# A decoder layer: the feed-forward norm vector is multiplied onto token rows instead of weights, a second pair of token tiles is turned by VectorE through DRAM, and differences are made in place

## The chip, the cores and the metric

The kernel runs on one core of a Trainium2 chip. The metric is the device time of one execution in microseconds. The engines have short names in the profile: PE is TensorE, DVE VectorE, ACT ScalarE, POOL GpSimd, SP SyncE; PEld are the weight loads of PE. SP issues nearly all transfers between DRAM and on-chip memory (SBUF); PE writes to PSUM, its own result memory.

## What is computed

One layer of a decoder over 1024 tokens of 1024 channels, in float32: a mixer (sparse attention of eight heads beside a short convolution) and a feed-forward part. The change lies in the feed-forward part and in what prepares it:

```python
mixed = jnp.concatenate([rms_norm(attn_out, g_out[l, :ATTN_WIDTH]),
                         rms_norm(conv_out, g_out[l, ATTN_WIDTH:])], axis=-1)
x = x + mixed @ w_o[l]
h = rms_norm(x, g_ffn_norm[l])
x = x + jnp.square(jax.nn.relu(h @ w_up[l])) @ w_down[l]
```

`rms_norm(x, g)` divides each token's row by its root mean square and multiplies channel by channel with `g`. Since `h @ w_up` sums over channels, `g_ffn_norm` may stand on the rows of `x` or on the rows of `w_up`. The matrix `w_up` is 1024 x 4096.

## The kernel before

**Tiles and stages.** Tokens are cut in eight tiles of 128, numbered 0 to 7. The stages are: the input projection (tiles `zp`, up to 139 us), the convolution part (`zX`, `zZ`, `zW`, up to 254 us), the convolution's share of the output projection (`wc`, up to 312 us, beside the first scores), attention tile by tile in the order 3, 2, 1, 0, 4, 5, 7, 6 (`ORDER`), the up projection with its square (545 to 880 us) and the down projection (to the end). Each float32 product is made of three fast ones: both operands are split in a rounded part and a rest (`hi` and `lo`, `copy_act` on ACT and a subtraction on DVE or POOL), and `mm3` issues three matmuls.

**Attention.** For each token tile and each of two groups, `scores` lets PE write pieces `s_` to two PSUM banks; DVE reduces each piece to `pt` with its minimum `nm` (an instruction pair that order rows call ISA), which frees the bank for the next piece. POOL and ACT weigh `pt`; PE transposes it (`tp`), ACT and DVE split it (`ph`, `pl`), and PE multiplies it with the values (`ot`). The keys come from DRAM as `kn00`, `kn10`, `kn01`, `kn11` (second digit: first or second half of the tokens), are rounded to `KH` by ACT, and their rests `KL` are made by DVE. The values `vs` and `vw` are 1024 KB each.

**The rows for the feed-forward part.** `finish` (L1476) ends a token tile: it adds the output projection `wa` to the residual row tile `y` (`yacc[tb]`, 128 x 1024), squares it for the norm, and scales it by `rffn`, one number per token. The up projection is a fast product of 2 x 2 blocks with seven products in place of eight. Its seven operands on the token side, `B11`, `B21`, `T1`, `T2`, `T3`, `B22`, `T4`, are halves of the rows of tokens 0 to 3 ("early") and 4 to 7 ("late") and their differences; `mate` pairs token tile 4 with 0, 5 with 1 and so on. Each must lie with channels on partitions, so each half row must be turned. `turn` (L1567) does this with four PE transposes of 128x128 to PSUM, from where ACT and DVE split it. For a pair in `BY_DRAM` (before: tiles 0 and 4), `finish` has DVE turn blocks of 32x32 of the whole row, writes it to DRAM (`t_d`) and reads it back in four pieces, so that it comes back turned; `side` (L1580) then only splits it, out of SBUF. The last token tile, 6, is handled in `second_half` (L1687): its row `ylast` is scaled to two half tiles `xn`.

**Norm vector.** `up_raw` (L1609) loads two of the 32 column blocks of `w_up` (`wu`, 1024 KB) and has ACT scale each of its eight row blocks by `g_ffn_norm`, which lies channel by partition in `cols`.

**What sets the order.** Nothing is issued in the order of the code. Class `Plan` records every operation, and `schedule` places them on the engines by a list schedule with priorities; these come from a backward pass (`latest`), and `best` shakes them once for each number in `SEEDS`: `shaken` moves the due times of the operations in one stretch of 5 to 40 us by random amounts. The result is one fixed order for each engine, with semaphores between engines. A new `SEEDS` therefore gives a new order for nearly everything.

Of the kernel before, what the change touches and what calls it, by code (L numbers as in the profile page):

```python
# [39 lines left out]
BY_DRAM = (0,)  # L40
# [1854 lines left out]
```

## Time and profile before

| | |
|---|---|
| median of 3 runs | 1191.03 us (1188.57 to 1192.53) |
| profiled execution | 1190.73 us |
| its span, first to last instruction | 1189.0 us |
| granted clock of PE, mean | 0.997 |
| data moved by the DMA engines | 161.28 MB |

The page gives busy times by engine. The span of a profiled execution is a little shorter than its time, by what lies ahead of the first instruction and behind the last one. Rows of groups read: engine, operation, tile written, tiles read, shape, count, and durations. In a view of one tile the three numbers are the least, the median and the greatest duration in nanoseconds. In a view of waits they are the total, the number of waits and the longest, in microseconds.

### The profile page before, as it was taken

How to read it: one execution, taken by the hardware profiler on the slowest of the kernel's cores; microseconds unless marked ns; L12 is line 12 of the kernel's file. 1: busy time of each engine (PE TensorE's matmuls, PEld its weight loads, DVE VectorE, ACT ScalarE, POOL GpSimd, SP SyncE). 2: the span in 40 equal slices, each digit the busy share in tenths (PEclk: the TensorE clock that was granted, in tenths of full speed). 3: DMA queues.
4: the chain of work that ended last, by engine and by line, in shares of the span. 5: the costliest groups of instructions: out<-in, count | busy, mean ns of one | idle time of the engine just before them, and what ended most of it. 6: DMA issues, size and time to landing. Idle time of an engine off the chain costs nothing.

```text
span 1189.0 us, 18003 instructions
## 1 busy us (share of the span) xinstructions
PE 1176.9 (99%) x5766; PEld 979.4 (82%) x5766; DVE 916.3 (77%) x1827; ACT 700.7 (59%) x1550; POOL 722.9 (61%) x663
## 2 busy tenths in 40 slices
PE   9999999999999999999999999999999999999998
PEld 7888878887878888888788888888888888888887
DVE  8868877785789999998985664554478979887875
ACT  7877635453689988888855554546345444444441
POOL 1544400022266554545878888787799999888971
PEclk9999999999999999999999999999999999999999
DMA  9845521268121101104045445353469545453513
GB/s 342 207 140 169 176 56 48 71 137 249 45 72 46 45 28 63 55 18 141 20 170 193 134 158 186 116 185 113 171 223 388 147 145 175 162 169 100 175 45 141
DMA packets 115102, 161.28 MB, mean 136 GB/s; under 512 B 21472, under 2 KB 68960, under 8 KB 115008
## 3 DMA queue, kind: packets, MB, share of 16 engines
q1 hardware_dynamic: 108752, 152.44, 39.8%
q10 hardware_dynamic: 5520, 5.28, 1.3%
q0 software_dynamic: 736, 2.43, 0.7%
q8 instruction: 45, 0.74, 0.2%
q14 instruction: 49, 0.40, 0.1%
HBM read 111.87 MB, written 48.23 MB: 135 GB/s over the span
## 4 chain that ended last, share of the span: by engine, by line
PE 89%; DVE 4%; ACT 4%; DMA 2%; issue 1%; SPq 0%; POOL 0%; POOLq 0%; ACTq 0%
PE X L273 28%; PE Z L273 18%; PE zp L273 9%; PE zX L273 5%; PE ot L273 5%; PE tp L273 4%; PE wa L273 3%; PE W L273 3%; PE zZ L273 3%; PE wc L273 2%; PE zW L273 1%; DMA w_raw<-in_w_in_dram 1%; PE hp L273 1%; ACT wu L273 1%; DVE pl L273 1%; DMA vs<-v_ds 1%
## 5 line engine op out<-in xcount | busy, mean ns | idle before, releaser
L273 PE MATMUL X<-we,uu 128*128 128x512 f32 (+1 forms) x726 | 200.9, 388 | 0.0
L273 PE MATMUL Z<-we,uu 128*128 128x512 f32 (+1 forms) x576 | 166.2, 388 | 0.0
L273 PEld LDWEIGHTS X<-we,uu 128*128 128x128 f32 x726 | 136.0, 188 | 28.2 <-DVE y L273 0.2
L273 ACT ACTIVATE uu<-ur 128x512 fp32r<-128x512 f32 x108 | 67.2, 629 | 122.0 <-PE Z L273 72.0
L273 PEld LDWEIGHTS Z<-we,uu 128*128 128x128 f32 x576 | 107.9, 188 | 22.3
L273 DVE TENSOR_TENSOR y<-X,y 128x512 f32<-128x512 f32 x129 | 87.1, 683 | 33.2 <-PE X L273 32.3
L273 ACT ACTIVATE pt<-pt,nm 128x640 f32<-128x640 f32 (+7 forms) x128 | 93.7, 734 | 29.9 <-DVE nm L273 29.7
L273 POOL TENSOR_TENSOR d<-d 128x512 f32<-128x512 f32 x64 | 98.8, 1562 | 8.4 <-DVE d L273 7.8
L273 DVE TENSOR_TENSOR pl<-tp,ph 128x512 fp32r<-128x512 f32 (+1 forms) x148 | 94.8, 656 | 7.5 <-ACT ph L273 7.0
L273 PE MATMUL tp<-ident,pt 128*128 128x128 f32 x528 | 93.0, 274 | 0.0
L273 ACT ACTIVATE ph<-tp 128x512 fp32r<-128x512 f32 (+1 forms) x148 | 80.9, 573 | 15.5 <-PE tp L273 11.5
L273 POOL TENSOR_TENSOR uu<-ur,uu 128x512 fp32r<-128x512 f32 x54 | 80.8, 1501 | 4.9 <-ACT uu L273 4.9
L273 ACT ACTIVATE we<-s 128x512 fp32r<-128x512 f32 x55 | 34.8, 632 | 81.5 <-PE X L273 40.4
L273 DVE TENSOR_TENSOR y<-Z,y 128x512 f32<-128x512 f32 x96 | 64.9, 681 | 21.2 <-PE Z L273 20.7
L273 PEld LDWEIGHTS tp<-ident,pt 128*128 128x128 f32 x528 | 67.5, 141 | 11.2 <-PE tp L273 0.3
L273 POOL MEMSET Qz<- 64x512 f32 x16 | 8.3, 521 | 107.0 <-PE zZ L273 102.9
L273 PE MATMUL zp<-w_lo,hTh 128*128 128x512 f32 (+1 forms) x192 | 67.0, 362 | 0.0
L273 PE MATMUL zp<-w_hi,hTh 128*128 128x512 f32 (+1 forms) x192 | 66.6, 363 | 0.1
L273 PE MATMUL zp<-w_hi,hTl 128*128 128x512 f32 (+1 forms) x192 | 66.0, 360 | 0.0
L273 DVE TENSOR_TENSOR we<-wu,we 128x512 fp32r<-128x512 f32 x38 | 48.5, 1290 | 20.5 <-PE X L273 10.8
L273 POOL TENSOR_TENSOR we<-wd,we 128x512 fp32r<-128x512 f32 x32 | 48.1, 1502 | 24.7 <-ACT we L273 24.3
L273 POOL TENSOR_TENSOR pt<-pt,rr 128x640 f32<-128x640 f32 (+4 forms) x64 | 62.9, 1009 | 0.0
(1353 smaller groups left out, 3611.5 us busy)
## 6 DMA issues: line engine op xcount, KB each, us to landing
u_d<-d SPq DMA_DIRECT2D x112, 256.0 KB, 3.3
ur<-u_d SPq DMA_DIRECT2D x108, 256.0 KB, 2.7
wu<-in_w_up_dram SPq DMA_DIRECT2D x16, 1024.0 KB, 5.8
wd<-in_w_down_dram SPq DMA_DIRECT2D x16, 1024.0 KB, 7.2
xt<-in_x_dram SPq DMA_DIRECT2D x10, 512.0 KB, 5.9
x<-in_x_t_dram SPq DMA_DIRECT2D x16, 256.0 KB, 6.2
w1r<-in_w_cmp_dram SPq DMA_DIRECT2D x16, 256.0 KB, 3.0
q_d<-qn SPq DMA_DIRECT2D x8, 512.0 KB, 3.0
```

Source lines behind the costliest of these rows:

```text
L273: node.do.append(lambda: getattr(engine, method)(*[real(x) for x in a], **{k: real(x) for k, x in kw.items()}))
```

## The change

`g_ffn_norm` comes as a new input `g_rows`, the vector repeated on 128 partitions. The 128 scalings of `wu` are left out. In their place every row is multiplied by the vector: on POOL behind ACT's scaling for token tiles 3 and 2 (in place) and for 1, 0, 4 and 5 (on the way to `yn`), on DVE in one instruction with the scaling for tile 7, and on DVE for tile 6, whose halves of the vector are loaded once more as `gh`. `BY_DRAM` now holds the pairs 1 and 0, so tiles 1 and 5 too go through DVE's transposes and DRAM. For tiles 4, 5 and 7 the difference behind `T2` is written over the one behind `T1`, where a tile `t` of its own was used; its pool `ez` is gone, and several small tiles have two buffers instead of three. `SEEDS` is another list.

```diff
-BY_DRAM = (0,)
+BY_DRAM = (1,0)
...
-SEEDS = (1, 23, 31, 38, 41, 62, 71, 73, 75, 77, 80, 88,
...
+SEEDS = (14, 20, 30, 31, 41, 47, 68, 70, 71, 73, 77, 92,
...
-def trunk_layer(ctx, tc, x, x_t, vectors, w_in, g_qk, w_cmp1, b_cmp1, w_cmp2, b_cmp2,
+def trunk_layer(ctx, tc, x, x_t, vectors, g_rows, w_in, g_qk, w_cmp1, b_cmp1, w_cmp2, b_cmp2,
...
-    cols = cst.tile([P, 68], F32, name="cols")
+    cols = cst.tile([P, 60], F32, name="cols")
...
-    G_MIX, G_FFN, G_OUT, CONV0, PE0 = 0, 8, 16, 24, 36
+    G_MIX, G_OUT, CONV0, PE0 = 0, 8, 16, 28
     def rsqrt(o, ss, n, scale):
-        t = st.tile([P, n], F32, name="rs_t", tag=f"rs{n}")
+        t = st.tile([P, n], F32, name="rs_t", tag=f"rs{n}", bufs=2)
...
-            ss = st.tile([P, G], F32, name="kss")
+            ss = st.tile([P, G], F32, name="kss", bufs=2)
-            ri = st.tile([P, G], F32, name="kri")
+            ri = st.tile([P, G], F32, name="kri", bufs=2)
...
-            ss = st.tile([P, H], F32, name="qss")
+            ss = st.tile([P, H], F32, name="qss", bufs=2)
-            ri = st.tile([P, H], F32, name="qri")
+            ri = st.tile([P, H], F32, name="qri", bufs=2)
...
-            e = st.tile([P, 3 * H], F32, name="ge")
+            e = st.tile([P, 3 * H], F32, name="ge", bufs=1)
...
+        g_ffn = pq.tile([P, D], F32, name="g_ffn", bufs=1)
         def load_wo():
+            nc.sync.dma_start(g_ffn, g_rows)
...
             if tb % 4 not in BY_DRAM:
-                if tb != ORDER[-1]:
+                if tb == ORDER[-2]:
+                    nc.vector.scalar_tensor_tensor(x1, x1, rffn[:, tb:tb + 1], g_ffn, op0=ALU.mult, op1=ALU.mult)
+                elif tb != ORDER[-1]:
                     copy_act(x1, x1, scale=rffn[:, tb:tb + 1])
+                    tt(nc.gpsimd, x1, x1, g_ffn, ALU.mult)
                 return
-            copy_act(yn.rearrange("p (c k t) -> p k c t", c=4, k=KD), x1.rearrange("p (k c t) -> p k c t", c=4, k=KD),
-                     scale=rffn[:, tb:tb + 1])
+            copy_act(x1, x1, scale=rffn[:, tb:tb + 1])
+            tt(nc.gpsimd, yn.rearrange("p (c k t) -> p k c t", c=4, k=KD), x1.rearrange("p (k c t) -> p k c t", c=4, k=KD),
+               g_ffn.rearrange("p (k c t) -> p k c t", c=4, k=KD), ALU.mult)
             nc.vector.transpose(x1, yn)
...
-        ez = pool(e_, "ez")
...
-        def first_turns(tb, t2):
-            tt(nc.vector, t2, rows[tb][1], rows[mate(tb)][0], ALU.subtract)
-            side("T2", tb, t2)
-            side("T1", tb, rows[mate(tb)][0])
+        def first_turns(tb, t2=None):
+            if t2 is None:
+                t2 = rows[mate(tb)][0]
+                side("T1", tb, t2)
+                tt(nc.vector, t2, rows[tb][1], t2, ALU.subtract)
+                side("T2", tb, t2)
+            else:
+                tt(nc.vector, t2, rows[tb][1], rows[mate(tb)][0], ALU.subtract)
+                side("T2", tb, t2)
+                side("T1", tb, rows[mate(tb)][0])
             tt(nc.gpsimd, rows[mate(tb)][1], rows[mate(tb)][1], t2, ALU.subtract)
...
             nc.sync.dma_start(raw, wuv[:, :, q * 2 * P:(q + 1) * 2 * P])
-            for k in range(KD):
-                copy_act(raw[:, k], raw[:, k], scale=cols[:, G_FFN + k:G_FFN + k + 1])
             return {f"A{i + 1}{j + 1}": raw[:, 4 * j:4 * j + 4, i * P:(i + 1) * P] for i in range(2) for j in range(2)}
...
         for tb in late[:-1]:
         for tb in late[:-1]:
-            t = ez.tile([P, 512], F32, name="t", tag="t")
-            first_turns(tb, t if tb % 4 not in BY_DRAM else t.rearrange("p (b k t) -> p b k t", b=4, k=4))
+            first_turns(tb)
             side("T3", tb, rows[tb][0])
...
+        gh = [temp("gh") for _ in range(2)]
+        for i in range(2):
+            nc.sync.dma_start(gh[i], g_rows[:, i * 512:(i + 1) * 512])
-        for o, a in zip(xn, halves(tb)):
-            nc.vector.tensor_scalar(o, a, rffn[:, tb:tb + 1], None, op0=ALU.mult)
+        for o, a, g in zip(xn, halves(tb), gh):
+            nc.vector.scalar_tensor_tensor(o, a, rffn[:, tb:tb + 1], g, op0=ALU.mult, op1=ALU.mult)
...
-_INS = ['x', 'x_t', 'vectors', 'w_in', 'g_qk', 'w_cmp1', 'b_cmp1', 'w_cmp2', 'b_cmp2', 'w_o', 'w_up', 'w_down']
+_INS = ['x', 'x_t', 'vectors', 'g_rows', 'w_in', 'g_qk', 'w_cmp1', 'b_cmp1', 'w_cmp2', 'b_cmp2', 'w_o', 'w_up', 'w_down']
-    a["vectors"] = np.concatenate([a[n].reshape(-1, P) for n in ("g_mix_norm", "g_ffn_norm", "g_out", "conv_w", "pe_cmp")]).T
+    a["vectors"] = np.concatenate([a[n].reshape(-1, P) for n in ("g_mix_norm", "g_out", "conv_w", "pe_cmp")]).T
+    a["g_rows"] = np.tile(a["g_ffn_norm"].reshape(-1), (P, 1))
     return a
```

Since the order is new, it shows best on the engines. The first place is in SP's queue, where the last keys are loaded at the beginning of attention (`kn01`, `kn11` keys, `vs` values, `y` and `xt` residual rows of 512 KB, `qx` queries of 64 KB). Before:

```order
L273 DMA xt_3052<-in_x_dram 128x1024
L273 DMA kn01_2920<-k_d0_211 32x16x64 x3
L273 DMA kn11_2921<-k_d1_210 32x16x64
L273 DMA vs_2942<-v_ds_209 128x8x256
L273 DMA y1_3079<-in_x_dram 128x1024
L273 DMA qx_3082<-q_d_215 32x4x128 x2
L273 DMA kn11_2921<-k_d1_210 32x16x64
L273 DMA kn01_2920<-k_d0_211 32x16x64
L273 DMA qx_3082<-q_d_215 32x4x128
L273 DMA kn11_2921<-k_d1_210 32x16x64 x2
```

And now, at the same place of SP's queue:

```order
L273 DMA kn01_2917<-k_d0_202 32x16x64 x4
L273 DMA xt_3067<-in_x_dram 128x1024
L273 DMA y1_3069<-in_x_dram 128x1024
L273 DMA kn11_2918<-k_d1_201 32x16x64
L273 DMA y0_3091<-in_x_dram 128x1024
L273 DMA qx_3022<-q_d_206 32x4x128
L273 DMA kn11_2918<-k_d1_201 32x16x64 x2
L273 DMA qx_3022<-q_d_206 32x4x128 x3
L273 DMA kn11_2918<-k_d1_201 32x16x64
L273 DMA y4_3148<-in_x_dram 128x1024
L273 DMA vs_2939<-v_ds_200 128x8x256
```

The values `vs` moved from ahead of the last keys to behind them, and the row tile `y0` from behind them to ahead.

The second place is on DVE, at the rests of those keys (`KL`), between the reductions (ISA rows) of the score pieces of token tile 3. Before:

```order
L273 ISA pt_3038,nm_80<-s__3156,d_sw_2937 128x256
L273 ISA nm_80 128x1
L273 TENSOR_TENSOR KL_2938<-kn01_2920,KH1_2939 64x512
L273 TENSOR_TENSOR KL_2938<-kn01_2920,KH0_2940 64x512
L273 TENSOR_TENSOR KL_2938<-kn11_2921,KH1_2939 64x512
L273 TENSOR_TENSOR KL_2938<-kn11_2921,KH0_2940 64x512
L273 ISA pt_3038,nm_80<-s__3176,d_sw_2937,nm_80 128x256
L273 ISA nm_80 128x1
L273 SCALAR_TENSOR_TENSOR y2_2923<-wc_3169,rconv_64,y2_2923 128x512
L273 ISA pt_3038,nm_80<-s__3182,d_sw_2937 128x512
```

And now, on DVE at the same score pieces:

```order
L273 ISA pc_3055,nm_80<-s__3163,d_c_2933 128x64
L273 ISA nm_80 128x1
L273 TENSOR_TENSOR KL_2935<-kn11_2918,KH0_2937 64x512
L273 TENSOR_TENSOR KL_2935<-kn11_2918,KH1_2936 64x512
L273 ISA pt_3053,nm_80<-s__3195,d_sw_2934,nm_80 128x256
L273 ISA nm_80 128x1
L273 SCALAR_TENSOR_TENSOR y2_2920<-wc_3181,rconv_64,y2_2920 128x512
L273 ISA pt_3053,nm_80<-s__3202,d_sw_2934 128x512
L273 ISA nm_80 128x1
L273 ISA pt_3054,nm_80<-s__3220,d_sw_2934 128x256
```

Two of the four rests moved further ahead; the two of `kn11` still stand before the reduction that frees a bank for the tenth piece (`s__3210` before, `s__3220` now).

The third place is on DVE near the end of attention, among the last `pl` (`y_3193` and `y_3102` are the rows of tokens 4 and 0). Before:

```order
L273 TENSOR_TENSOR t<-y_3193,y_3102 128x512
L273 TENSOR_TENSOR pl<-tp,ph 128x512
L273 TENSOR_TENSOR B11l<-tp,B11h 128x4x128
L273 TENSOR_TENSOR pl<-tp,ph 128x512 x2
L273 TENSOR_SCALAR rs_t<-ss 128x1
L273 TENSOR_TENSOR B21l<-tp,B21h 128x4x128
L273 TENSOR_TENSOR pl<-tp,ph 128x512 x3
L273 TENSOR_TENSOR we<-wu,we 128x512
L273 TENSOR_TENSOR B21l<-tp,B21h 128x4x128
L273 TENSOR_TENSOR pl<-tp,ph 128x512
```

And now (`y_3211` and `y_3069` are the rows of tokens 5 and 1, `y_3956` and `y_2919` those of 7 and 3, `y_3148` and `y_3091` those of 4 and 0):

```order
L273 TENSOR_TENSOR y_3069<-y_3211,y_3069 128x4x128
L273 TENSOR_TENSOR pl<-tp,ph 128x512
L273 TENSOR_TENSOR B21l<-tp,B21h 128x4x128
L273 TENSOR_TENSOR we<-wu,we 128x512
L273 TENSOR_TENSOR pl<-tp,ph 128x512 x3
L273 TENSOR_TENSOR B11l<-tp,B11h 128x4x128
L273 SCALAR_TENSOR_TENSOR y_3956<-y_3956,rffn,g_ffn 128x1024
L273 TENSOR_TENSOR B21l<-tp,B21h 128x4x128
L273 TENSOR_TENSOR pl<-tp,ph 128x512 x3
L273 TENSOR_TENSOR y_2919<-y_3956,y_2919 128x512
L273 TENSOR_TENSOR y_3091<-y_3148,y_3091 128x4x128
L273 TENSOR_TENSOR pl<-tp,ph 128x512
```

The multiplication of tokens 7 and three differences now stand between the last `pl`, where before there was one difference.

More of the change, by code (lines that the diff above doesn't have):

```diff
@@ L150, in __init__ @@
         self.seen, self.nodes, self.tile = [], [], None
-SEEDS = (1, 23, 31, 38, 41, 62, 71, 73, 75, 77, 80, 88, 104, 105, 109, 117, 124, 125, 127, 128, 139, 177, 192, 197, 199, 200, 266, 277, 284, 301, 314, 374, 375, 379, 394, 395, 403, 428, 451, 473, 489, 497, 527, 539, 602, 635, 663, 668, 683, 688, 735, 738, 757, 795, 807, 960, 974, 981, 1033, 1087, 1174, 1207, 1227, 1240, 1266, 1330, 1456, 1463, 1494, 1514, 1524, 1530, 1663, 1704, 1707, 1772, 1800, 1878, 2113, 2223, 2390, 2423, 2489, 2544, 2549, 2570, 2574, 2706, 2765, 2808, 2860, 2976, 2978, 3198, 3470, 3483, 3569, 3710, 3726, 3799, 3961, 4024, 4169, 4173, 4281, 4302, 4454, 4464, 4536, 4631, 4816, 4942, 5475, 5732, 5800, 5998, 6019, 6274, 6308, 6361, 6542, 6590, 6629, 6638, 6652, 6763, 6768, 6849, 6898, 6926, 6933, 7427, 7431, 7843, 8840, 8935, 9098, 9312, 9425, 9449, 9490, 9543, 9796, 10243, 10373, 10450, 10719, 10753, 10755, 10988, 11031, 11263, 11298, 11337, 11378, 11468, 11734, 11858, 11860, 12512, 12525, 12556, 12899, 12910, 12948, 13367, 13696, 13855, 13915, 13972, 14164, 15272, 15349, 15386, 15617, 16147, 16281, 16952, 16985, 17425, 17652, 17676, 17915, 18093, 18097, 18255, 18325, 18342, 18702, 18971, 19150, 19474, 19616, 21193, 21235, 21388, 21680, 21948, 22334, 23213, 23339, 23611, 23843, 24118, 24207, 24710, 24756, 24876, 25684, 25805, 26155, 26173, 26856, 27014, 28405, 28909, 29650, 29975, 30412, 30442, 30461, 30772, 31961, 32809, 33604, 33968, 34207, 35108, 35382, 35516, 35716, 35789, 36229, 36353, 36557, 36875, 38880, 39359, 39872, 39943, 39989, 40863, 40948, 40951, 41904, 43210, 43597,)
@@ new lines @@
+SEEDS = (14, 20, 30, 31, 41, 47, 68, 70, 71, 73, 77, 92, 103, 104, 125, 131, 139, 164, 184, 197, 198, 204, 206, 208, 214, 252, 265, 269, 277, 278, 287, 292, 309, 344, 353, 364, 403, 416, 504, 552, 560, 615, 616, 705, 736, 862, 906, 931, 933, 970, 1019, 1021, 1059, 1066, 1265, 1270, 1292, 1319, 1350, 1370, 1441, 1450, 1455, 1456, 1459, 1467, 1516, 1751, 1835, 1838, 1908, 1911, 1986, 2096, 2163, 2183, 2238, 2546, 2570, 2992, 3096, 3181, 3198, 3602, 3603, 3928, 3965, 4011, 4057, 4068, 4116, 4127, 4235, 4239, 4955, 4985, 5129, 5230, 5273, 5560, 5669, 5709, 5757, 5766, 5889, 6051, 6275, 6349, 6504, 6567, 6935, 6974, 7011, 7022, 7151, 7232, 7236, 7309, 7650, 7676, 7699, 7930, 8052, 8504, 8561, 9021, 9025, 9356, 9362, 9731, 9939, 10335, 10637, 10848, 11058, 11189, 11302, 11336, 11348, 11351, 11364, 11371, 11822, 12383, 12673, 13340, 13751, 13970, 14031, 15022, 15458, 15492, 15584, 15699, 15725, 15913, 15991, 16733, 17230, 17824, 17915, 18026, 19187, 19713, 19731, 19987, 20003, 20346, 20365, 20475, 21312, 22541, 23629, 24017, 24232, 24507, 24756, 25167, 26647, 26909, 27025, 27176, 27256, 27359, 27761, 27839, 28399, 28427, 28437, 28641, 28744, 28919, 29124, 29257, 29664, 29829, 29977, 30497, 30542, 30772, 31439, 32106, 32733, 34667, 34852, 35229, 35311, 35378, 35807, 36058, 36542, 37299, 37916, 40155, 40512, 40671, 40697, 42002, 42697, 43651, 44218, 44538, 44556, 44953, 45141, 46791, 46992, 48676, 48683, 48716, 49199, 51370, 51435, 51519, 53813, 53823, 53979, 55232, 55424, 56021, 56381, 56945, 57898, 59781, 59848, 61066, 61963,)
```

## The prediction

> **What bounds the kernel now.** I read the page first: the busy shares, then the chain that ended last, then who TensorE (PE) waited for.
>
> ```profile
> span 1189.0 us, 18003 instructions
> ...
> PE 1176.9 (99%) x5766; PEld 979.4 (82%) x5766; DVE 916.3 (77%) x1827; ACT 700.7 (59%) x1550; POOL 722.9 (61%) x663
> ...
> PE 89%; DVE 4%; ACT 4%; DMA 2%; issue 1%; SPq 0%; POOL 0%; POOLq 0%; ACTq 0%
> ...
> PE s__3210 L273 <- DVE nm L273: 2.2, 1, 2.2
> ...
> PE s__3861 L273 <- DVE nm L273: 1.4, 1, 1.4
> PE ot L273 <- DVE pl L273: 1.0, 2, 0.7
> PE tp L273 <- DVE t L273: 0.8, 1, 0.8
> ...
> PE Z L273 <- DVE B22l L273: 0.4, 1, 0.4
> ```
>
> The first three rows are the page, the others the view of waits for PE alone. PE is busy 99% of the span, 89% of the chain is PE, and its largest waits sum to about 6 us. A busy PE need not be a full one, so I looked at start-to-start times: in the feed-forward part a 128x512 matmul follows the last one every 0.23 us, without a break. So the time is PE's work plus a few waits, and an instruction taken off PE is worth its slot, unless a wait takes that slot.
>
> The windows show where something else is close to becoming the limit, and where PE's clock fell (columns: stretch, length, busy time of PE, weight loads, DVE, ACT, POOL, then granted clock, DMA share, GB/s).
>
> ```profile
> 268.00:272.00 4.00, 4.00 (x21) 3.34 (x21) 3.30 (x14) 1.52 (x4) 0.62 (x1) 1.00 1.10 342
> 272.00:276.00 4.00, 4.00 (x20) 3.35 (x19) 2.34 (x9) 1.31 (x3) 0.00 (x0) 1.00 1.17 292
> ...
> 278.00:281.00 3.00, 1.02 (x5) 0.46 (x4) 1.75 (x4) 1.15 (x2) 0.00 (x0) 1.00 1.06 353
> 281.00:285.00 4.00, 3.82 (x12) 3.12 (x13) 2.62 (x11) 2.57 (x6) 1.21 (x2) 0.57 1.07 379
> ...
> 340.00:342.00 2.00, 2.00 (x9) 1.71 (x7) 1.58 (x8) 1.13 (x5) 2.00 (x5) 0.50 0.33 93
> ...
> 410.00:460.00 50.00, 50.00 (x310) 43.48 (x309) 47.28 (x158) 44.72 (x98) 24.68 (x37) 1.00 0.13 46
> ...
> 541.00:587.00 46.00, 44.52 (x259) 36.91 (x257) 41.77 (x67) 41.38 (x88) 35.87 (x33) 1.00 0.31 104
> ...
> 600.00:700.00 100.00, 100.00 (x442) 82.48 (x441) 68.33 (x66) 58.06 (x117) 84.16 (x56) 1.00 0.51 174
> 700.00:880.00 180.00, 180.00 (x794) 148.35 (x793) 93.24 (x104) 87.83 (x169) 143.91 (x97) 1.00 0.45 152
> ```
>
> Three places matter. **Late keys**: at 278.6 PE waits 2.2 us, and for about 3.4 us behind it the clock is halved (0.57 over four microseconds). The second large wait, at 336, is followed in the same way (0.50 at 340 to 342). **Attention**: PE is full, but DVE has 47.3 of 50 us. **The turn to the feed-forward part**, 541 to 587: PE 44.5, DVE 41.8 and ACT 41.4 of 46. From 600 on nothing but PE counts.
>
> **The transposes that go.** 84 transposes of 128x128 become 56: tokens 1 lose two operands, tokens 5 five, of four blocks each. Their price is in the timeline:
>
> ```profile
> 592.01 0.62 PE L273 MATMUL X<-T2h,we 128*128 128x512 f32 x2
> 592.47 0.60 PE L273 MATMUL tp<-ident,y 128*128 128x128 f32 x4
> 592.82 0.48 PE L273 MATMUL X<-T2l,we 128*128 128x512 f32 x1
> 593.13 0.63 PE L273 MATMUL X<-T2h,we 128*128 128x512 f32 x2
> ```
>
> From 592.47 to 593.13 PE does four transposes and one matmul. The pair at 592.01 took 0.46, so a matmul is 0.23 and four transposes 0.43 (not the 0.60 shown, which holds the pipeline's tail). Seven such groups are 7 x 0.43 = **3.0 us** less for PE. This is the only change in PE's work.
>
> **The scalings of the weights that go.** 128 ACT instructions disappear:
>
> ```profile
> L273 ACT ACTIVATE wu<-wu,cols x128: 492/497/526, 549.7 to 825.0; 128x256 f32<-128x256 f32 x128
> ```
>
> At 0.5 us, 64 us of ACT at most. Behind 600 they lie beside a PE at 100.00 of 100.00 and 180.00 of 180.00: worth nothing. The 24 of the first three weight blocks stand at 549.7 to 573.4, some 10 us of an ACT that is nearly full there; what they free is weighed below.
>
> **The multiplications that come.** Tokens 3, 2, 1, 0, 4 and 5 get a multiplication of 128x1024 on POOL, tokens 7 one on DVE, tokens 6 two halves on DVE where a plain scaling stood. Nearest rows:
>
> ```profile
> L273 POOL TENSOR_TENSOR y<-y,t x4: 1284/1292/1762, 552.9 to 586.9; 128x512 f32<-128x512 f32 x4
> ...
> L273 DVE TENSOR_TENSOR t<-y,y x3: 680/1119/1768, 549.2 to 573.3; 128x512 f32<-128x512 f32 x3
> ...
> L273 DVE SCALAR_TENSOR_TENSOR d<-d x48: 678/1066/1794, 598.2 to 880.8; 128x512 f32<-128x512 f32 x48
> ...
> L273 DVE TENSOR_SCALAR xn<-ylast,rffn x2: 1516/1540/1565, 579.0 to 581.7; 128x512 f32<-128x512 f32 x2
> ...
> L273 DVE STREAM_TRANSPOSE y<-yn x2: 1234/1235/1236, 456.4 to 497.3; 128x1024 f32<-128x1024 f32 x2
> ```
>
> POOL: twice 1.28 to 1.76, so 2.6 to 3.5 us each, about 16 us in all. POOL is half idle in attention (24.7 of 50), so I cost them at nothing; if that cover fails, the price is the DVE work held up, in the third rival. The two halves for tokens 6 cost 0.68 to 1.79 against 1.54 before: between 1.7 us gained and 0.5 lost on the last chain; I take nothing. The two transposes more on DVE are 2 x 1.2 us, one of them around 430 and one around 520, where DVE idles 2.7 us in 50: hidden, or 2.4 us. ACT's count for the rows falls by one. The 512 KB of row vectors fall at 310 to 320 and the two half tiles near 575, and the DRAM round trips of tokens 1 and 5 end long before use: two legs of 2.8 us at the median.
>
> ```profile
> L273 SPq DMA_DIRECT2D t_d<-y x2: 338/384/430, 458.0 to 498.6; - x2
> ...
> DMA to landing us min/median/max: 2.4/2.8/3.3
> ```
>
> **The turn to the feed-forward part.** Counted from the last scores to the last tokens' `t2`, PE's work there stays at 43 us; but on DVE six reads of PSUM (0.60 from start to start) become six operations on SBUF alone. These rows show what such reads cost:
>
> ```profile
> 580.45 0.68 DVE L273 TENSOR_TENSOR T4l<-tp,T4h 128x512 fp32r<-128x512 f32 x1
> 581.05 0.68 DVE L273 TENSOR_TENSOR B22l<-tp,B22h 128x512 fp32r<-128x512 f32 x1
> ...
> L273 DVE TENSOR_TENSOR T1l<-y,T1h x1: 681/681/681, 578.4 to 578.4; 128x512 fp32r<-128x512 f32 x1
> ...
> L273 DVE TENSOR_TENSOR T4l<-y,T4h x1: 1826/1826/1826, 591.9 to 591.9; 128x512 fp32r<-128x512 f32 x1
> ```
>
> The same operation takes 0.68 when POOL is out of the way and up to 1.83 beside a POOL operation. So DVE gains 0 to 6.6 us of work; at the middle of the rows (1.12 for `t<-y,y`) 3 us. It idles 4.2 us of these 46, mostly waiting for ACT, which now has 10 us less. I take the two as even and add **0**. The bounds: if DVE no longer holds PE, the 1.9 us of PE's waits here go; if all 6.6 come, DVE has 48.4 where there were 46, and PE stands some 3 us longer. In the program, tokens 7's 128x1024 multiplication stands ahead of three `pl`, for which the next `ot` waits; the wait of 0.7 us on `pl` in the list above is of that kind.
>
> **The late keys.** SyncE's queue has a new order. In the trace of before `vs`, 1024 KB, is issued ahead of the last key loads, and the loads start when PE is done with `zZ` (last row, from SyncE's waits):
>
> ```profile
> 264.06 1.97 SPq L273 DMA_DIRECT2D vs<-v_ds  x1
> 266.13 1.02 SPq L273 DMA_DIRECT2D y<-in_x_dram  x1
> ...
> 268.16 0.95 SPq L273 DMA_DIRECT2D kn<-k_d  x2
> ...
> 270.37 2.79 SPq L273 DMA_DIRECT2D kn<-k_d  x2
> ...
> SPq L273 <- PE zZ L273: 3.8, 1, 3.8
> ```
>
> DVE then stands at the key rests `KL`, the reduction that frees a score bank stands behind them, and PE waits for that bank. In the new order `vs` comes behind the keys, and one row tile of 512 KB and one `qx` of 64 KB come ahead: 448 KB less. At 292 to 342 GB/s the last key lands 1.3 to 1.6 us sooner. But PE comes sooner too: both programs put the same 84 `wc` matmuls and nine score pieces ahead of the wait, and behind the last `zZ` only 7 other matmuls where there were 12. That is 5 x 0.23 less two transposes, 0.9 us. So the wait shrinks from 2.2 to about 1.6: **0.6 us** gained. The halved clock costs half of 3.4 us, 1.7; the wait at 336, listed at 1.4 us, had it too, so I keep it. Bounds: 3.9 gained (no wait, full clock) to 0.9 lost (no earlier landing).
>
> A page reads this differently. The Trainium skill, "TensorE: Matmul & The Clock Gate", section "HAM oscillation — how this bites in real kernels", gives as its abstract rule no idle gaps of PE over about 3.4 us. By it a wait of 2.2 us would leave the clock alone; the rows above (1.02 busy of 3 us, then 0.57) speak against it, and the measurement decides. By the page's rule the most that the keys could give is 2.2 instead of 3.9.
>
> **The sum.** The profiled execution took 1190.73 us, 1.73 more than its span; the median of the three runs is 1191.03, so the two agree. 1190.73 - 3.0 - 0.6 + 0 = **1187.1 us**.
>
> **Rivals.** *Given back*: DVE becomes the bound at the turn, and the 3.0 us come back as waits of PE for `pl`, `T2l` or `T1l`. For it: DVE has 41.8 of 46 and grows; PE already waits there. Against it: ACT's 10 us. Time: 1190.1.
>
> *Keys in time*: the queue clears faster than its bytes say, because the `vs` and `y` issues also held SyncE for 3 us; wait and half clock both go, 3.9 in place of 0.6. Time: 1183.8.
>
> *POOL holds DVE*: each of the six long POOL multiplications stops a DVE operation on SBUF, and with it the reductions and `pl` queued behind, which PE needs within a microsecond. By the rows (0.68 alone, up to 1.83) a 128x512 POOL operation costs up to 1.1 us; one twice as long up to 2.6, 15.6 for six. It decides the sign once more than 3.6 us reach PE. At half, 7.8: 1194.9. Against it: `pl` and the score reductions read PSUM, and in the groups of the trace `pl` never exceeds 0.69. The Trainium skill, "SBUF — State Buffer", section "SBUF: two separate sides", states just this mechanism: the port pair of VectorE and GpSimd is an exclusive lock, and the loser "fully blocks". The two-input rows above agree (0.68 to 1.83), and by that rule the six could cost the whole 15.6.
>
> ```profile
> L273 DVE TENSOR_TENSOR pl<-tp,ph x148: 406/686/694, 313.3 to 558.6; 128x512 fp32r<-128x512 f32 x132, 128x256 fp32r<-128x256 f32 x16
> ```
>
> That the change does not do what it says I exclude: the program has 28 transposes fewer.
>
> **How the numbers follow.** Forecast 0.45 (1185.3 to 1188.9), given back 0.26, keys in time 0.22, POOL holds DVE 0.07. A measurement of this kernel tells about 0.3%, 3.6 us, from no change; faster means below 1187.5. That takes the keys' 0.22 and somewhat over half of the forecast's 0.45: 0.48. Slower means above 1194.6: 0.06. The rest, 0.46, is the same. The range reaches from beyond the keys' case, at 1182, past given back with its bound, to 1192.
>
> **What would show it.** Right: 56 transposes in the trace, PE still at 99% and full from 600 on; a wait before the tenth score piece of about 1.6 us and two stretches of halved clock; PE's waits between 541 and 600 summing to about 2 us. Given back shows as 4 to 5 us of them there, with `pl` or the rests of `T1`, `T2` as releasers. Keys in time shows as one stretch of halved clock, not two. The lock shows as waits of PE on `nm` or `pl` between 360 and 545, where there are none now. Most likely to make this wrong: the new order moves nearly all instructions of the first 550 us, and a wait that no row here shows may stand anywhere in them.

## The result, and the profile after

The changed kernel takes 1199.54 us (median; 1198.30 to 1201.47), the kernel before 1190.46 us in the same session: ratio 1.0085, 95% interval 1.0071 to 1.0099. It is **slower by about 9 us** (0.85%), where 1187.1 with 1182 to 1192 was predicted. Its profiled execution took 1198.33 us, 7.6 more than the one of before. One execution of the last run below took 2372.13 us; its ratio leaves that one out. First the page of the changed kernel (span, busy times, chain), then its waits of PE:

```profile
span 1196.5 us, 17861 instructions
...
PE 1178.7 (99%) x5738; PEld 976.7 (82%) x5738; DVE 926.4 (77%) x1830; ACT 649.3 (54%) x1421; POOL 743.4 (62%) x669
...
PE 84%; DVE 6%; DMA 5%; ACT 2%; issue 1%; POOL 1%; SPq 1%; ACTq 0%; DVEq 0%; POOLq 0%
```

```profile
PE s__3876 L273 <- DVE nm L273: 2.0, 1, 2.0
PE s__3220 L273 <- DVE nm L273: 2.0, 1, 2.0
PE hp L273 <- ACT ah L273: 1.9, 1, 1.9
PE warm L273 <- POOL ident L273: 1.4, 1, 1.4
PE tp L273 <- DVE pl L273: 1.3, 2, 1.1
PE zX L273 <- ACT ta L273: 1.2, 1, 1.2
PE zp L273 <- ACT hTh L273: 1.1, 2, 0.7
```

PE has its 28 instructions fewer (5766 to 5738), and yet it is busy longer, because a busy PE can do less: from 73 to 78 us, at a mean granted clock of 0.66, it is busy for 4.90 us with 18 instructions, where the kernel before, at full clock, has 28 in 5.00. The chain lost five points of PE to DVE and DMA. Three of the waits are new, and they lie at 7 to 11 us (`zp`), 71 (`hp`) and 146 (`zX`): in the input projection and the convolution, **where the change has no operation at all**.

The windows show it by what PE got done. The x number is the count of instructions in the stretch; before, then the changed kernel:

```profile
0.00:250.00 250.00, 247.77 (x1220) 206.65 (x1221) 198.28 (x407) 154.11 (x430) 59.78 (x82) 1.00 0.49 146
```

```profile
0.00:250.00 250.00, 243.95 (x1190) 202.06 (x1191) 196.06 (x398) 149.77 (x426) 62.15 (x82) 0.99 0.48 144
...
285.00:288.00 3.00, 1.04 (x8) 0.67 (x6) 2.60 (x6) 2.23 (x6) 0.00 (x0) 1.00 1.04 325
288.00:293.00 5.00, 5.00 (x18) 4.01 (x17) 1.82 (x8) 1.35 (x5) 0.61 (x1) 0.66 1.12 308
...
548.00:594.00 46.00, 43.99 (x237) 35.46 (x237) 41.14 (x63) 30.15 (x60) 35.84 (x31) 1.00 0.38 124
...
600.00:700.00 100.00, 99.98 (x442) 82.20 (x442) 76.01 (x72) 38.13 (x67) 83.53 (x55) 1.00 0.49 166
700.00:880.00 180.00, 180.00 (x795) 148.73 (x794) 96.17 (x103) 69.58 (x118) 144.59 (x98) 1.00 0.45 150
```

In its first 250 us PE started 30 instructions fewer on the same work; at 0.227 us each that is 6.8 us. From 600 us on nothing changed. The loss is early, with a part at the turn.

To put a number on each stage I took from the trace, for every PE instruction, the time to the next one's start, less the slot that its width takes where PE is full (0.227 us for 512 columns, 0.114 for 256, 0.109 for 128). The few other widths got a slot of their own in the same way. What is left is PE's **excess**: waits, halved clock, and whatever else delays a start.

| stretch | before | changed | difference |
|---|---|---|---|
| 0 to 250 us | 9.7 | 16.5 | +6.8 |
| 250 to 550 us | 20.3 | 21.6 | +1.3 |
| 550 to 650 us | 3.6 | 5.9 | +2.3 |
| PE's own slots, whole span | 1148.1 | 1145.0 | -3.1 |

With 0.2 at the end that is the 7.5 us by which the span grew. The first row, the largest, was missing from the prediction. It is one profile of each kernel; how far it is chance shows below.

### The profile page after: what moved, and what is told of

It reads as the page before. It is cut to its first block, busy times and chain, and to the rows that moved or that the text cites. A ratio compares the mean times of both kernels' runs of the same rounds, so it can differ in the third digit from the quotient of the medians.

```text
span 1196.5 us, 17861 instructions
## 1 busy us (share of the span) xinstructions
PE 1178.7 (99%) x5738; PEld 976.7 (82%) x5738; DVE 926.4 (77%) x1830; ACT 649.3 (54%) x1421; POOL 743.4 (62%) x669
## 4 chain that ended last, share of the span: by engine, by line
PE 84%; DVE 6%; DMA 5%; ACT 2%; issue 1%; POOL 1%; SPq 1%; ACTq 0%; DVEq 0%; POOLq 0%
PE X L273 29%; PE Z L273 18%; PE zX L273 5%; PE ot L273 5%; PE tp L273 5%; PE zp L273 4%; PE wa L273 3%; PE W L273 3%; PE zZ L273 3%; PE wc L273 2%; PE zW L273 1%; DMA k_d<-kturn 1%; DMA kn<-k_d 1%; DMA w_raw<-in_w_in_dram 1%; DVE pl L273 1%
## 5 line engine op out<-in xcount | busy, mean ns | idle before, releaser
L273 DVE TENSOR_TENSOR y<-X,y 128x512 f32<-128x512 f32 x129 | 87.1, 683 | 33.5 <-PE X L273 32.8
L273 DVE TENSOR_TENSOR we<-wu,we 128x512 fp32r<-128x512 f32 x38 | 50.5, 1349 | 20.6 <-PE X L273 15.8
L273 ACT ACTIVATE we<-wu 128x512 fp32r<-128x512 f32 x57 | 35.7, 631 | 53.8 <-PE X L273 43.0
```

The lines of the kernel that those rows point to most:

```text
L273: node.do.append(lambda: getattr(engine, method)(*[real(x) for x in a], **{k: real(x) for k, x in kw.items()}))
```

## The experiments

Two theories stand against each other. **O, the order**: the planner's new seeds gave every stage another order, and the early one is worse. **W, the work**: something that the change does (a second pair through DRAM, products on POOL, smaller buffers) causes the waits. To move an order from one program to another I used that the planner sorts by due times: a table `EARLY` sets them for chosen operations to those of the other program's plan. The first 3323 recorded entries are the same in both programs, so the mapping is exact there.

```diff
-        end, order = self.schedule(self.best(SEEDS)[1])
+        late = list(self.best(SEEDS)[1])
+        for k, v in enumerate(np.frombuffer(zlib.decompress(base64.b85decode(EARLY)), np.int32)):
+            if v >= 0:
+                late[k] = v / 100 - 100
+        end, order = self.schedule(late)
```

All results in one table. The kernel before ran beside each group, with medians of 1189.1 to 1191.1, so the ratio to it is the column to compare. The last three columns are PE's excess in us, of one profile each; two programs with the same order differ there by 1 us or more. All programs with the changed kernel's early order, whatever their arithmetic, have 15.6 to 17.5 in the first 250 us (`one_move`, with one place of it changed, 15.2); those with almost the early order of before and the small buffers have 10.3 to 12.7, and the kernel before has 9.7.

| run | us | ratio, 95% interval | 0-250 | 250-550 | 550-650 |
|---|---|---|---|---|---|
| changed kernel | 1199.54 | 1.0085 (1.0071-1.0099) | 16.5 | 21.6 | 5.9 |
| early_of_before | 1192.20 | 1.0018 (1.0003-1.0033) | 11.3 | 20.8 | 5.7 |
| early_of_after | 1211.71 | 1.0188 (1.0157-1.0219) | 16.0 | 27.7 | 10.2 |
| small_buffers | 1211.90 | 1.0181 (1.0147-1.0216) | 12.6 | 32.8 | 10.2 |
| one_pair | 1213.42 | 1.0197 (1.0167-1.0228) | 16.6 | 27.0 | 11.2 |
| buffers_alone | 1191.97 | 1.0010 (0.9998-1.0022) | 12.7 | 19.4 | 3.0 |
| order_of_before | 1202.30 | 1.0086 (1.0069-1.0103) | 11.4 | 24.2 | 12.7 |
| one_pair_fixed | 1208.36 | 1.0143 (1.0123-1.0163) | 17.5 | 21.6 | 11.5 |
| scalings_back | 1200.23 | 1.0075 (1.0060-1.0090) | 16.2 | 20.7 | 8.5 |
| one_move | 1195.88 | 1.0049 (1.0034-1.0064) | 15.2 | 20.6 | 5.9 |
| turn_moves | 1193.97 | 1.0038 (1.0025-1.0050) | 10.3 | 22.8 | 6.0 |
| score_move | 1192.56 | 1.0027 (1.0016-1.0037) | 10.8 | 21.8 | 5.7 |
| all_moves | 1194.00 | 1.0034 (1.0022-1.0046) | 12.1 | 20.8 | 6.9 |
| early_of_after_fixed | 1200.22 | 1.0082 (1.0063-1.0102) | 15.6 | 25.7 | 3.2 |
| no_products | 1199.51 | 1.0081 (1.0060-1.0101) | 11.3 | 21.9 | 10.5 |
| no_products_apart | 1198.90 | 1.0070 (1.0050-1.0090) | 11.6 | 25.5 | 9.3 |
| no_vector_buffers | 1198.66 | 1.0073 (1.0055-1.0090) | 12.2 | 23.5 | 9.2 |
| before_one_move | 1192.71 | 1.0032 (1.0020-1.0043) | 15.0 | 18.2 | 3.8 |
| same_order_no_products | 1193.19 | 1.0035 (1.0021-1.0049) | 11.0 | 22.0 | 5.7 |

### Whose early order

> The changed kernel, with the due times of the first 2271 operations (all that the plan of before starts in its first 262 us) taken from the plan of before, so that these stand almost in the order of before; its arithmetic and its smaller `st` buffers are those of the changed kernel. Between the two profiles PE's excess over its instructions' own slots rose from 9.7 to 16.5 us in the first 250 us, where the change has no operation. Theory O, the order (the planner's seeds were drawn anew, and another order of the same work made the waits at 70.8 and 146.3 us and the halved clock at 73.8): the 6.8 us go, time 1198.3 - 6.8 = 1191.5 (1190 to 1193), no stretch of halved clock before 250 us. Theory W, the change's own work (smaller buffers, the second pair of tiles, six POOL products): the early waits stay, 1197 to 1200.

> The kernel before, with the `st` buffers cut as in the change (kss, kri, qss, qri, rs_t to 2, ge to 1) and the due times of the first 2273 operations (262 us) from the changed kernel's plan; its arithmetic, transposes and scalings of weights are those of before. Theory O: it inherits the 6.8 us, 1190.7 + 6.8 = 1197.5 (1196 to 1199), with a halved clock near 74 us after a wait of hp for ah. Theory W: 1190 to 1192, since none of the change's operations is in it but the buffers.

The first is O: 1192.2, and the intervals of the two ratios lie apart. The two programs have the same arithmetic and the same buffers, so this pair shows the order by itself: 7.3 us of time, 5.2 of early excess (16.5 to 11.3). PE's instructions in the first 250 us:

```profile
0.00:250.00 250.00, 246.96 (x1213) 205.57 (x1214) 197.70 (x404) 154.38 (x430) 60.03 (x82) 1.00 0.47 145
```

1213, against 1190 and 1220. The second is a miss by size: the early excess came as expected (16.0), but the program also lost 14 us behind 250. The seeds shake due times by where operations stood in the plan, so with other buffers they shake other operations, and a list that had been chosen for one program is chance for any other. The same happened in the two runs that went with it:

```diff
-            ss = st.tile([P, G], F32, name="kss")
+            ss = st.tile([P, G], F32, name="kss", bufs=2)
...
-BY_DRAM = (1,0)
+BY_DRAM = (0,)
```

> The kernel before with the `st` buffers cut as in the change and the due times of the first 262 us from its own plan of before, so that the buffers alone differ and the order moves little. Theory O: 1190 to 1192. Rival B, the buffers (a wait for one of two buffers where there were three): the early excess rises by up to 6.8 us, 1195 to 1198, with waits of PE before 250 us.

> The changed kernel with BY_DRAM = (0,): the second pair of tiles goes back to TensorE (84 transposes instead of 56), the norm vector stays on the rows; by the program's order the first 392 us stay as in the changed kernel, instruction for instruction. Theory O: the early 6.8 us stay, and PE has 28 transposes or 3.0 us more, less what the turn lost (PE's excess between 550 and 600 us rose from 3.5 to 5.5): 1198.3 + 3.0 - 2.0 = 1199.3, up to 1201.4 if the turn's loss isn't the pair's. Theory W, with the pair as its cause: below 1196.

Both were inconclusive on what they were made for: 1211.9 and 1213.4, with the loss behind 250 us. From here on I fixed the later due times too.

> The kernel before with the `st` buffers cut as in the change, and now all due times (9792 operations) fixed to those of its own plan, so that its order stays nearly that of before to the end; `small_buffers` lost it after 262 us. Theory O (the order alone cost the 6.8 us): 1190.4, between 1189.5 and 1191.5. Rival B (the smaller buffers cost): PE's excess in the first 250 us, 9.7 us before, goes to 12 or more as in `small_buffers`, time 1193 or more.

> The kernel before with the changed kernel's small `st` buffers, the due times of the first 2273 operations (262 us) from the changed kernel's plan and all later ones fixed to its own plan: its first quarter stands almost in the order of the changed kernel, the rest in that of before. Its arithmetic is that of before. Theory O: PE's excess in the first 250 us goes from 9.7 to about 16, time 1190.5 + 6.8 = 1197.3 (1195 to 1198.5; the late keys may take up 1 to 2 of it, as in `buffers_alone`). If the change's operations are needed for the loss: 1190 to 1192.

`buffers_alone` is 1.0010, with 1 inside the interval. Its early excess did rise, to 12.7, but 0.9 us came back between 250 and 550 (the late keys' wait fell to 0.6) and 0.6 at the turn: net, by the interval, the buffers cost between nothing and 2.6 us. This run does not show the buffers by themselves: with them the order moved a little too (some 30 of DVE's first 380 instructions stand elsewhere than in the kernel before). `early_of_after_fixed` is the mirror of the first run: the arithmetic of before, in the early order of the changed kernel, takes 1200.2. That is above the expected 1195 to 1198.5; 4.4 of it stand between 250 and 300 us, at the seam of the two orders. Without those it would be near 1196. Its early excess is 2.9 above that of `buffers_alone`, which has the same buffers. PE's wait at the place taken up next is there too:

```profile
PE hp L276 <- ACT ah L276: 1.5, 1, 1.5
```

None of the change's operations is in this kernel, only its small buffers. So the second pair and the products fall as causes of the early loss, and **3 to 5 us of the 6.8 are the order's**. The rest, 1.6 us in `early_of_before` and 3.0 in `buffers_alone` above the kernel before, is the buffers, the little that moved in the order with them, or chance; the runs do not part these.

### One place of the order

What is wrong with it? In the timeline of DVE, the rows are start, duration, operation, count, and in brackets the idle time ahead and its releaser. Before:

```profile
65.65 0.31 DVE L273 STREAM_TRANSPOSE kturn<-krow 128x128 f32<-128x128 f32 x1 [3.19 <-DMA k_d<-kturn]
...
67.97 0.69 DVE L273 TENSOR_TENSOR z<-z,qri 128x512 f32<-128x512 f32 x1
68.58 0.68 DVE L273 TENSOR_TENSOR araw<-tp,cols 128x512 f32<-128x512 f32 x1
69.18 0.70 DVE L273 STREAM_TRANSPOSE zT<-z 128x512 f32<-128x512 f32 x1
```

The changed kernel, DVE, then ACT:

```profile
66.78 0.31 DVE L273 STREAM_TRANSPOSE kturn<-krow 128x128 f32<-128x128 f32 x1 [4.08 <-DMA k_d<-kturn]
...
69.10 0.69 DVE L273 TENSOR_TENSOR z<-z,qri 128x512 f32<-128x512 f32 x1
69.82 0.71 DVE L273 STREAM_TRANSPOSE zT<-z 128x512 f32<-128x512 f32 x1
71.02 0.76 DVE L273 TENSOR_TENSOR qn<-zT,qn 128x256 fp32r<-128x256 f32 x2 [0.48 <-ACT qn L273]
71.70 0.68 DVE L273 TENSOR_TENSOR araw<-tp,cols 128x512 f32<-128x512 f32 x1
```

```profile
72.42 0.63 ACT L273 ACTIVATE ah<-araw 128x512 fp32r<-128x512 f32 x1 [1.12 <-DVE araw L273]
```

In both, DVE stands for 3 to 4 us at a `kturn` whose buffer a transfer `k_d` still reads, and everything queued behind stands with it. Then it has a backlog. Before, `araw`, which PE needs by way of `ah`, starts 0.6 us after `z`; in the changed kernel it comes behind `zT` and two `qn`, 2.6 us after `z`. PE waits 1.9 us, and its clock is halved for 3.4 us behind that. `qn` goes to DRAM, and its first reading back (`qx`) is at 259 us. To test that this place alone makes the wait, I moved it out of the changed kernel and, backwards, into the kernel before (`MOVES` edits the finished order by the numbers of the operations: 841 to 846 are `zT`, the `qn` and `q_d`, 774 is `araw`, 775 `ah`):

```diff
+MOVES = (((841, 842, 843, 844, 845, 846), 'after', 775),)
```

```diff
+MOVES = (((841, 842, 843, 844, 845), 'before', 774),)
```

> The changed kernel with one place of its order edited by hand: `zT<-z`, the four `qn` and their transfer `q_d` go behind the `araw` and `ah` that they stood ahead of (six operations moved behind two), nothing else. In the changed kernel DVE came free of its wait for `k_d` at 66.8 us and ran `zT` and two `qn` (69.8 to 71.7) ahead of `araw`, PE waited 1.95 us for `ah`, and its clock was halved for 3.4 us from 73.8. Theory O, with this place as its costliest: `araw` starts near 69.8, `ah` lands near 71.2, PE's wait falls below 0.3 us and the halved clock (1.7 us) goes: 1199.5 - 3.6 = 1195.9 (1195 to 1197). Rival: the loss only moves to the next operand in the same queue (`qn`, the next `araw`): 1198 or more.

> The kernel before with the move of `one_move` made backwards: `zT<-z` and the four `qn` go ahead of the first `araw` (which DVE ran at 68.6 us, straight behind `z`), all else in its order. Theory O: `araw` starts 2 to 3 us later, at 71 or so, `ah` lands near 72, PE's first `hp` at 70.8 waits 1 to 2 us and its clock may be halved for 3.4 us: 1190.5 + 1.5 = 1192.0, or 1193.7 with the halved clock; if the late keys' wait at 278.6 takes up part of it, 1191. Rival, the place is harmless by itself: 1190.5 within 0.5.

Both came out in the time; by the mechanism only the second did. `one_move` takes 1195.88, where 1195.9 stood, but its profile does not show why. `araw` starts at 70.00, and `hp` 1.7 us sooner than in the changed kernel, but PE, arriving earlier too, still waits 1.3 where less than 0.3 was expected:

```profile
PE hp L274 <- ACT ah L274: 1.3, 1, 1.3
```

The halved clock at this place is gone, but it is gone in `scalings_back` too, whose `araw` was left where it stood (a wait of 2.1). The early excess fell by 1.3 of the 3.6 us expected, and another 1.0 went between 250 and 550. The wait is the shortest of its kind, as the six programs that keep the changed order here wait 1.5 to 2.5, but not by much. So in this direction the time is as forecast and the cause is not shown. `before_one_move` is 3.6 us slower than the kernel before in its session (1189.13). Its early excess rose by 5.3, of which 2.1 came back between 250 and 550. DVE's rows and the wait:

```profile
70.49 0.71 DVE L274 STREAM_TRANSPOSE zT<-z 128x512 f32<-128x512 f32 x1
71.68 0.76 DVE L274 TENSOR_TENSOR qn<-zT,qn 128x256 fp32r<-128x256 f32 x2 [0.48 <-ACT qn L274]
72.36 0.69 DVE L274 TENSOR_TENSOR araw<-tp,cols 128x512 f32<-128x512 f32 x1
```

```profile
PE hp L274 <- ACT ah L274: 2.3, 1, 2.3
```

In this direction the cause is shown: a place without a wait got one of 2.3 us and a halved clock behind it. So one reversal among some 18000 instructions can cost about as much as the 28 transposes give (3.6 us, 2.4 to 5.1 by the interval).

### The scalings, the pair and the whole order

```diff
+            for k in range(KD):
+                copy_act(raw[:, k], raw[:, k], scale=ones)
```

> The changed kernel with 128 ACT scalings of the up weights put back, by 1.0 from a column of ones, and the due times of all other operations fixed to its own. The prediction took them as hidden: from 600 us on PE stays full and the time is 1199.5, within 1.0. Rival: 24 of them (about 10 us of ACT) stand before 600 us and hold up the splits at the turn: PE's excess from 550 to 650 rises from 5.9 to 8 or more, time 1202 or more.

> The changed kernel with BY_DRAM = (0,) as in `one_pair` (84 transposes on TensorE), its due times fixed to those of the changed kernel where both have the operation (9601 of 9673), so that the order holds beyond 392 us. If the second pair is worth its 3.0 us of PE and costs nothing at the turn: 1199.5 + 3.0 = 1202.5. If it gives back what the turn lost (2.0): 1200.5. If it costs more than it saves: 1199 or less. New waits where the 72 operations without a fixed place fall may add a little.

> The changed kernel with the due times of all operations that both have in common and that the plan of before starts in its first 545 us (5188) taken from the plan of before. Theory O: against the changed kernel the early 6.8 us and the 1.3 us that the stretch from 250 to 550 lost (20.3 to 21.6) go: 1199.5 - 8.1 = 1191.4; with the turn's loss alone left it is 1190.7 - 3.0 + 2.1 = 1189.8; so 1189 to 1192. Rival, the pair and the in-place differences cost at the turn whatever the order: the excess from 550 to 600 stays at 5.3 or more. If instead the turn's loss was the order's too, it is back at 3.5 and the time at 1187.7, near the prediction.

The 128 scalings cost nothing that the times can tell: 1.0075 against 1.0085. The one profile does show 2.6 us more excess at the turn, as the rival had it, and 1.2 less ahead of it; the rival's 1202 was not reached. The other two miss. With the second pair on PE again the time is 1208.4, 9 us more, of which 3.1 are transposes and 5.6 stand at the turn, with a wait of PE of 2.4 us for a `T2l`; 72 operations had no fixed place. And `order_of_before` gained 5.1 early and lost 6.8 at the turn (PE waits 2.6 us for a row `y`) and 2.6 between. In both the turn was planned anew from a beginning for which no seeds had been chosen. They say little of the pair, and much of the turn: replanning it costs 3 to 7 us.

### The turn

Now `early_of_before` is the base. In its turn, POOL and ACT:

```profile
585.76 2.21 POOL L276 TENSOR_TENSOR xn<-xn 128x512 f32<-128x512 f32 x1 [2.87 <-DVE xn L276]
587.93 1.74 POOL L276 TENSOR_TENSOR s<-wu 128x512 f32<-128x512 f32 x1
```

```profile
589.71 0.63 ACT L276 ACTIVATE we<-s 128x512 fp32r<-128x512 f32 x1 [0.24 <-POOL s L276]
```

PE waits 0.9 us for that `we`. It looks like the place at 70 us: an operation that could run stands behind one that waits.

```diff
+MOVES = (((7240,), 'before', 7217), ((7350,), 'after', 6951), ((6968,), 'after', 6840))
...
+MOVES = (((3753,), 'before', 3749),)
```

> `early_of_before` (1192.2) with three operations moved at the turn to the feed-forward part: POOL's first `s<-wu` ahead of the `xn` that waits 2.9 us for DVE; POOL's `wu<-wu` behind the `sq` that PE's `ssa` waits for; DVE's first `we<-wu,we` (1.79 us beside POOL instead of 0.68) behind two `pl` that PE waits for. If the turn's 2 us are the order's: PE's waits there (1.0 for `we`, 0.6 for `sq`, 1.0 for `pl`) go, 1192.2 - 2.6 = 1189.6 (1189 to 1190.5), excess from 550 to 600 from 5.3 to 3. If they are the operations' own, POOL's products and the in-place differences being one chain too many: other waits take their place, 1191.5 or more.

> `early_of_before` with one DVE operation moved: the mask and row maximum of the score piece `s__3791` goes ahead of that of `s__3731`, so that its bank comes free some 3 us earlier. PE waits 2.0 us for that bank at 339.2 (`s__3876` <- DVE `nm`), a wait that the kernel before, the changed one and all variants have, and its clock is halved for 3.4 us after it. Expected: wait below 0.5 and no second stretch of halved clock, 1192.2 - 1.6 - 1.7 = 1188.9 (1188 to 1190). Rival: DVE is the bound there, the wait moves to the next piece, 1191.5 or more.

> `early_of_before` with the moves of `turn_moves` and `score_move` together. If both hold, they add up, as they lie 200 us apart: 1192.2 - 2.6 - 3.3 = 1186.3 (1185 to 1188), below the kernel before (1190.5) by about the 3.0 us of PE's work that the change takes away. If either is taken back by another wait, 1188.5 or more.

Three misses, and alike: the waits aimed at went or shrank (`we` from 0.9 to 0.5), and another took their place. In `turn_moves` PE waits for `t` instead:

```profile
PE tp L277 <- DVE t L277: 1.3, 1, 1.3
PE X L277 <- ACT we L277: 0.5, 1, 0.5
PE tp L277 <- DVE pl L277: 0.4, 1, 0.4
```

The price stands in DVE's rows. POOL's `s`, moved ahead, now runs from 584.34 to 585.96, and two subtractions of DVE take 1.76 and 1.78 us, which took 0.68 each in `early_of_before`; the first lies beside that `s`, the second beside POOL's next operation. Here are both in `early_of_before`, then in `turn_moves`:

```profile
584.27 0.68 DVE L276 TENSOR_TENSOR y<-xn,y 128x512 f32<-128x512 f32 x1
...
586.14 0.68 DVE L276 TENSOR_TENSOR t<-xn,y 128x512 f32<-128x512 f32 x1
```

```profile
584.73 1.78 DVE L277 TENSOR_TENSOR y<-xn,y 128x512 f32<-128x512 f32 x1
...
587.69 1.76 DVE L277 TENSOR_TENSOR t<-xn,y 128x512 f32<-128x512 f32 x1
```

In `score_move` the next score piece waits 1.6 us in place of 2.0. At the turn DVE has little time to spare (44.5 of the 50 us from 550 on; 30.7 of 50 between 50 and 100 us in the changed kernel), so there, in these three tries, a move only chose who is late. None of these is faster than the kernel before. What remained were the change's own operations at the turn:

```diff
-                    tt(nc.gpsimd, x1, x1, g_ffn, ALU.mult)
```

> `early_of_before` (1192.2) without the six POOL products of the token rows with the norm vector (their rows miss the factor `g_ffn_norm`; the scalings stay), all other due times fixed to those of `early_of_before`. If the products cost at the turn (POOL late with `sq`, DVE slowed beside POOL): PE's excess from 550 to 600 us falls from 5.3 to 3.5, time 1190.4. If they are hidden, as predicted: 1191.5 to 1192.9.

> As `no_products`, and also without the tile of the norm vector (the row that DVE multiplies misses it too), whose room goes to a tile `t` of its own for the differences, as in the kernel before, in place of the in-place form. If the in-place form is what costs at the turn: PE's excess from 550 to 600 us is 1.5 to 2 lower than in `no_products`, time lower by as much, 1190.2 or less. If it costs nothing: within 0.7 of `no_products`.

> As `no_products`, without the tile of the norm vector, whose room goes to the `st` buffers: all back at the size of before; the differences stay in place. With before's early order as well: PE's excess of the first 250 us, 11.3 in `early_of_before` and 12.7 in `buffers_alone`, goes to that of before, 9.7, and the time is 1 to 2 lower than `no_products`. If the buffers cost nothing net (late keys take it up): within 0.7 of `no_products`.

Leaving the products out made it slower by 7 us, for the same reason as above: a new plan of the turn (10.5 in place of 5.7). The three are useless for what they were to tell. The last run kept the order word for word:

> `early_of_before` (1192.2) without the six POOL products of the token rows with the norm vector (those rows miss the factor `g_ffn_norm`), every other instruction of every engine in the order of `early_of_before`. If the products are hidden, as predicted: 1191.7 to 1192.7, PE's excess from 550 to 600 us stays at 5.3. If POOL's work on them is what costs (the lock on DVE, `sq` late): excess from 250 to 600 falls by 1.5 or more, time 1190.7 or less.

1193.2 against 1192.2, with overlapping intervals, and an excess at the turn of 5.7 as with them: leaving them out gains nothing, so **the six products are hidden**.

## Why the prediction was wrong

**The transposes, -3.0: right.** Twenty and eight fewer in the groups (64 to 44 `tp<-ident,y`, 12 to 4 `tp<-ident,t`), and PE's slots fell by 3.1 us.

**The scalings, 0, and the multiplications, 0: right** (`scalings_back` by its time, with a doubt of 2 us at the turn in its profile; `same_order_no_products`). The products, from the view of the vector's tile (least, median, greatest duration in ns; first and last start):

```profile
L273 POOL TENSOR_TENSOR yn<-y,g_ffn x4: 2405/2418/2430, 435.7 to 525.6; 128x1024 f32<-128x1024 f32 x4
L273 POOL TENSOR_TENSOR y<-y,g_ffn x2: 2410/2421/2432, 392.1 to 413.4; 128x1024 f32<-128x1024 f32 x2
```

2.42 us each where 2.6 to 3.5 stood. The rival "POOL holds DVE" falls for these six with the same run: leaving them out removed no wait. That a POOL operation can hold a DVE one is so, as `turn_moves` shows.

**The late keys, -0.6: wrong by that much.** A wait of 1.6 us was forecast; it is 2.0 at 285, with the clock halved behind it (0.66 from 288 to 293). The excess from 250 to 300 went from 5.4 to 5.3. The mechanism was right, and its two terms were both too small. Counted from the start of the last `zZ` (250.83 us before, 258.91 now), the last key landed after 27.8 us and now after 25.7, 2.1 sooner where 1.3 to 1.6 stood; PE came to the piece after 28.2 us and now after 26.5, 1.7 sooner where 0.9 stood. What was left of the gain is 0.2 of the wait.

**The turn, 0: wrong in size, inside its bound of 3.** It lost 2.3 us, which takes back most of the 3.0, as the rival "given back" had it, but its sign came out only in part: PE's listed waits from 550 to 650 went from 1.9 us, all for DVE, to 2.9, of which 1.5 are for DVE (`pl`), 0.8 for ACT (`we`) and 0.6 for POOL (`sq`). ACT did get its 10 us (30.2 of the 46 from 548 on, before 41.4 from 541 on, as the stage lies 7 us later); DVE stayed as full as it was (41.1, before 41.8). Which operation brings it was not settled: the products are cleared, and for the in-place differences and the second pair every variant replanned the turn and lost more than was to be measured.

**The step that failed** is the sum itself. It went over what the change removes, adds and moves on purpose, and let the first 250 us stand as in the trace of before. The text named the danger ("the new order moves nearly all instructions of the first 550 us") and priced it at nothing, in the sum and in the range. It measured +6.8 us, twice the transposes: with it, 1190.7 - 3.1 + 6.8 + 1.3 + 2.3 = 1198.0, beside the 1198.3 of the profiled execution. That the order makes 3 to 5 us of it is shown from both sides with the buffers held fixed: 16.5 to 11.3 (changed kernel, `early_of_before`), and 12.7 to 15.6 (`buffers_alone`, `early_of_after_fixed`). One place in it, `araw` behind `qn`, is shown in one direction, at 3.6 us in the kernel before; in the other the time came out and the wait did not. The rest of the 6.8 was not taken apart. The waits at 7 to 11 us are partly chance: `one_move`, with the same order there, has none of them. Nor were the 1.6 us explained that `early_of_before` keeps early: restoring the buffers (`no_vector_buffers`, 12.2) did not bring them back.

Would the change be worth it in a good order? `early_of_before` says no: with 28 transposes fewer it is still not faster than the kernel before (1.0003 to 1.0033). Against PE's 3.1 us stand 2.1 more excess at the turn, 1.6 early and 0.5 between.

## What to carry to other kernels

Where a change makes a planner place everything anew, the new order is a term of the sum: compare the order in stages that the change does not touch, look for an engine's backlog behind a transfer wait, and ask who comes out of it first, what PE needs or what is not needed yet. An order tuned for one program is chance for its neighbours (here mostly 1 to 2% slower), so a variant tests an operation only if the order of everything else is held fixed. And before moving an operation ask whether its engine has slack: at 70 us one reversal cost 3.6 us, at the turn three moves gained nothing. A time that comes out as forecast does not show the mechanism, as `one_move` does; look whether the wait went too.

## What the runs showed of the hardware

The granted clock falls on a **grid**. Every stretch of halved clock, but the one at each trace's very end, lasted 3.413 us or twice that (to 0.001), and within a profile the starts of such stretches lie whole multiples of 3.413 us apart: 281.578 and 339.604 before (17.0 of them), 73.806, 288.846 and 346.872 in the changed kernel (63.0 and 17.0). So the length of a wait does not decide by itself, but how much of it falls into one cell. I laid that grid on all twenty profiles, by the stretch at the end where there was no other. Cells in which PE idled 1.9 us or more were followed by half clock in 24 of 25 cases, cells with 1.46 to 1.9 in 5 of 17, cells with 0.9 to 1.45 in none of 47. Two stretches, in `buffers_alone` and `same_order_no_products`, followed a cell with 0.1 us of idle time, and what made them is open. The grid starts elsewhere in every execution, so the same wait of 2.0 us near 340 was followed by half clock in the changed kernel, at a cost of 1.7 us, and was not in `early_of_before`, where 1.6 us of it fell into one cell. That may be part of the spread of 3 us and more between executions of one kernel.

The Trainium skill, "TensorE: Matmul & The Clock Gate", Part 1, describes a free-running window of 3413 ns; the grid of 3.413 us agrees. The same page of the Trainium skill, section "HAM oscillation — how this bites in real kernels", gives as its rule no gaps over about 3.4 us. The measurement here is stricter, and it decides: 1.9 us within a cell were enough in 24 of 25 cases.
